# Score products with the low parts of the keys on 64 rows, head pairs on opposite halves of the array

## The chip, the cores and the metric

The kernel runs on one core of one Trainium2 chip. The metric is the device time of one execution in microseconds; three executions of the kernel before took 2033.07, 2031.86 and 2033.2 us, median 2033.07. The core's engines are TensorE (PE; its weight loads are listed apart as PEld), VectorE (DVE), ScalarE (ACT), GpSimd (POOL) and SyncE (SP), each with an instruction stream of its own. Matmul results go to PSUM, whose banks hold 512 float32 values per partition; other data lies in SBUF.

## The reference

One layer of a decoder block, 2048 positions, width 1024, float32. One projection of the normalized input gives the inputs of a gated short convolution, the queries, keys and values of a sliding-window attention (16 query heads, 4 key/value heads, head width 64, window 128), and gates. The change touches only the scores of the attention:

```python
    q = rms_norm(q.reshape(b, s, N_Q_HEADS, HEAD_DIM), q_norm_g)
    k = rms_norm(k.reshape(b, s, N_KV_HEADS, HEAD_DIM), k_norm_g)
    ...
    scores = jnp.einsum('bnqhgd,bnkhd->bnhgqk', qb.astype(jnp.float32),
                        kb.astype(jnp.float32)) * scale
    ...
    valid = (diff >= 0) & (diff < WINDOW) & (k_pos >= 0)
    scores = jnp.where(valid[None, :, None, None], scores, NEG_INF)
    ...
    m = jnp.maximum(jnp.max(scores, axis=-1, keepdims=True), sink)
    p = jnp.exp(scores - m)
    p = p / (jnp.sum(p, axis=-1, keepdims=True) + jnp.exp(sink - m))
    out = jnp.einsum('bnhgqk,bnkhd->bnqhgd', p.astype(v.dtype), vb)
```

Everything else (projections, convolution, gates, output projection, residual) is as usual for such a block and stays as it was.

## The kernel before

**Precision.** TensorE multiplies in a fast type (`F32R`) that keeps fewer bits than float32. So each operand is split into a high part, rounded to that type, and a low part, what is left. The large products (L364, `product`) take three matmuls for each: high by high, high by low, low by high; low by low is dropped.

**Layout.** The 2048 positions are worked in two tiles `t` of 1024. In each, units of 256 columns of the projections run one after another (`sunit`, L364, 512-column matmuls on 128 rows into the banks X, V and Y). Between the steps of these units the kernel places other work by hand: `put(n, f)` enters a piece of work for tick `n`, and `run` (each step of a unit is a tick) issues what is due after the unit's own matmuls. The order in each engine's stream is therefore written out by the program.

**Attention.** For each tile, key/value head `j` (4) and block `b` of 128 positions (8) there is one round of attention, 64 in all. A round is spread over ticks: `att_load` at n-4, `att_scores` at n, `att_exp` at n+1, `att_norm` at n+2, `att_turn` (four transposes, L779) at n+4, `att_values` (L809) at n+7, `att_out` at n+8. In the first half of a tile's rounds they are 5.25 ticks apart, in the second half 3.25.

**Queries and keys.** A key/value head serves four query heads, in two pairs `c` (the pair of 256-column halves `i` in `fin_q`), and in a pair two heads `e`. `fin_q` splits the queries into `hi` and `lo` and stores them by POOL's queue into `q2d`: `hi` in rows 0 to 63 (`LH`), `lo` in rows 64 to 127 (`UH`), the 64 rows being the head's 64 dimensions. `kd` holds the keys' high part (`l = 0`) and low part (`l = 1`), each written twice, to rows 0 to 63 and to rows 64 to 127. One matmul on 128 rows with `l = 0` thus gives q_hi k_hi + q_lo k_hi, and with `l = 1` it gives q_hi k_lo + q_lo k_lo.

**Scores.** `att_scores` makes eight matmuls, for `h` (half block of 64 positions), `c` and `l`, each with 128 columns of weights (64 positions times two heads) and 192 moving columns (keys of the window). Each matmul has its weight load, also where two in a row use the same weights. The result `sp` is one tile of two PSUM banks, indexed `[h, c]`, so that a half block has a bank. The pool `ps_s` has one buffer: the next round's first score matmul waits until the exponentials of this one have read theirs. Then VectorE writes the masked part (`copy_predicated`, L748; L744 and L746 in the rounds without earlier keys), takes the maximum (L750) and a few small steps, and ScalarE takes the exponentials, four of 128 columns (L763).

**Two small matmuls** in the beginning use fewer rows of the array: L163 (`prep_gain`, 8 rows, between the warming matmuls `clear`, L1098) and L168 (`prep_cols`, 42 rows).

Of the kernel before, what the change touches and what calls it, by code (L numbers as in the profile page):

```python
# [11 lines left out]
AF = mybir.ActivationFunctionType  # L12
ALU = mybir.AluOpType
AX = mybir.AxisListType

P = 128
# [9 lines left out]
HD = 64  # L26
# [12 lines left out]
LH, UH = slice(0, HD), slice(HD, P)  # L39
HALVES = (LH, UH)  # L40
# [3 lines left out]
def block_kernel(  # L44
# [15 lines left out]
    nc = tc.nc  # L60
# [18 lines left out]
    def slot(shape, dt, name):  # L79
        return big.tile(shape, dt, tag="big", name=name)  # L80
# [37 lines left out]
    for h in range(2):  # L118
        nc.gpsimd.affine_select(
            out=mask_f[:, h, :], in_=ones[:, 0:HD], pattern=[[1, HD]], compare_op=ALU.is_gt,  # L120
# [4 lines left out]
    negc = consts.tile([P, HD], F32, name="negc")  # L125
# [17 lines left out]
    rows = slot([NR, P], F32, "rows")  # L143
# [65 lines left out]
    def add(o, a, b, eng=None):  # L209
        return (eng or nc.vector).tensor_tensor(out=o, in0=a, in1=b, op=ALU.add)  # L210
# [4 lines left out]
    def mul(o, a, b, eng=None):  # L215
        return (eng or nc.vector).tensor_tensor(out=o, in0=a, in1=b, op=ALU.mult)
# [213 lines left out]
    def into(dst, val):  # L430
        if isinstance(val, tuple):
            add(dst, *val)
        else:
            nc.scalar.copy(dst, val)
# [115 lines left out]
    def put(n, f):  # L550
        at.setdefault(max(n, tick[0] + 1), []).append(f)
# [17 lines left out]
    def turn4(src, name):  # L569
        pt = mbank(name)  # L570
        for b in range(HB):
            nc.tensor.transpose(pt[:, b, :], src[:, b * P : (b + 1) * P], ident)
        return pt

    def head_square(pt, name):
        sq = pt.rearrange("p b q -> p (b q)")
        nc.scalar.activation(out=sq, in_=sq, func=AF.Square)
        return sq

    def head_reduce(sq, ss, n):  # L580
        nc.vector.tensor_reduce(
            out=ss[:, n * 8 : (n + 1) * 8], in_=sq.rearrange("p (h d) -> p h d", d=HD), axis=AX.X, op=ALU.add)

    def head_rms(ss, name):
        ms = small.tile([P, 32], F32, tag="sm", name=f"{name}_ms")
        nc.vector.tensor_scalar(out=ms, in0=ss, scalar1=1.0 / HD, scalar2=EPS, op0=ALU.mult, op1=ALU.add)
        return rsqrt(ms, 32, name)
# [3 lines left out]
    def fin_q(t, j):  # L591
        ss = small.tile([P, 32], F32, tag="ss", bufs=3, name=f"qss{t}_{j}")
        left = [4]

        def fin(i, q, val):
            nm = f"q{t}_{j}_{i}_{q}"
            qt = slot([P, H], F32, f"{nm}_t")
            into(qt, val)
            hi, lo = slot([P, H], F32R, f"{nm}_h"), slot([P, H], F32R, f"{nm}_l")
            nc.scalar.activation(out=hi, in_=qt, func=AF.Copy, scale=gqk)  # L600
            nc.vector.scalar_tensor_tensor(
                out=lo, in0=qt, scalar=gqk, in1=hi.bitcast(F32), op0=ALU.mult, op1=ALU.subtract)
            for e in range(2):
                for half, src in ((LH, hi), (UH, lo)):
                    nc.gpsimd.dma_start(
                        q2d[t][j][half, q * 2 * HB : (q + 1) * 2 * HB, i, e, :],
                        src[HALVES[e]].bitcast(F32).rearrange("p (b x) -> p b x", x=HD))

            def sums():
                sq = head_square(turn4(qt, f"pt{nm}"), nm)  # L610
                put(tick[0] + 1, lambda: reduce(sq))

            def reduce(sq):
                head_reduce(sq, ss, 2 * i + q)
                left[0] -= 1
                if left[0] == 0:
                    put(tick[0] + 1, rms)

            put(tick[0] + 1, sums)

        def rms():
            r = head_rms(ss, f"q{t}_{j}")

            rq = consts.tile([P, 2, HB, 2, 2], F32, tag="rq", bufs=4, name=f"rq{t}_{j}")
            rv = r.rearrange("p (c q b e) -> p q b c e", c=2, q=2, e=2)
            for e in range(2):
                for h in range(2):
                    nc.vector.tensor_copy(rq[HALVES[e], :, :, h, :], rv[HALVES[h], :, :, :, e])
            rqs[t, j] = rq

        return fin
# [75 lines left out]

    def att_load(t, j, b):  # L710
        nm = f"{t}_{j}_{b}"
        gb = t * NB + b
        q2 = slot([P, 2, 2, P], F32R, f"q2_{nm}")
        nc.sync.dma_start(
            q2.bitcast(F32).rearrange("p h c x -> p (h c x)"),
            q2d[t][j][:, 2 * b : 2 * b + 2].rearrange("p h c e x -> p (h c e x)"))
        k2 = slot([P, 2, 2 * P], F32R, f"k2_{nm}")
        if b > 0:
            nc.sync.dma_start(k2.bitcast(F32), kd[t][j, :, :, (b - 1) * P : (b + 1) * P])
        else:  # L720
            nc.sync.dma_start(k2[:, :, P:].bitcast(F32), kd[t][j, :, :, 0:P])
            if gb > 0:
                nc.sync.dma_start(k2[:, :, :P].bitcast(F32), kd[t - 1][j, :, :, T - P : T])
        v2 = slot([P, 4, P], F32R, f"v2_{nm}")
        nc.sync.dma_start(v2.bitcast(F32), vd[gb, :, :, j, :])
        return q2, k2, v2

    def att_scores(t, j, b, ld):
        first = t * NB + b == 0
        nm = f"{t}_{j}_{b}"  # L730
        q2, k2, _ = ld
        rv = rqs[t, j][:, b // HB, b % HB]
        sp = ps_s.tile([P, 2, 2, 2 * P], F32, tag="s", name=f"s{nm}")
        for h in range(2):
            skip = (2 - h) * HD if first else 0
            for c in range(2):
                for l in range(2):
                    nc.tensor.matmul(  # L738
                        sp[:, h, c, skip : 3 * HD], lhsT=q2[:, h, c, :],
                        rhs=k2[:, l, h * HD + skip : h * HD + 3 * HD], start=l == 0, stop=l == 1)  # L740
        sg = sp.rearrange("p h c k -> p (h c) k")
        m = mask_i.unsqueeze(1).to_broadcast([P, G, HD])
        if first:
            nc.vector.copy_predicated(  # L744
                sg[:, :, 2 * HD : 3 * HD], m, negc.unsqueeze(1).to_broadcast([P, G, HD]))
            nc.vector.tensor_copy(sg[:, 0:2, HD : 2 * HD], negc.unsqueeze(1).to_broadcast([P, 2, HD]))  # L746
        else:
            nc.vector.copy_predicated(sg[:, :, 2 * HD : 3 * HD], m, sg[:, :, 0:HD])  # L748
        st = small.tile([P, 6, G], F32, tag="st", name=f"st{nm}")
        nc.vector.tensor_reduce(out=st[:, 0], in_=sg[:, :, HD : 3 * HD], axis=AX.X, op=ALU.max)  # L750
        mul(st[:, 5].rearrange("p (h c) -> p h c", c=2), st[:, 0].rearrange("p (h c) -> p h c", c=2), rv)
        nc.vector.scalar_tensor_tensor(
            out=st[:, 1], in0=st[:, 5], scalar=-1.0, in1=nsink_r[:, j].rearrange("p h c -> p (h c)"),
            op0=ALU.mult, op1=ALU.min)
        add(st[:, 2], sink_r[:, j].rearrange("p h c -> p (h c)"), st[:, 1])
        return sg, st, rv

    def att_exp(t, j, b, got):
        sg, st, rv = got
        nc.scalar.activation(out=st[:, 3], in_=st[:, 2], func=AF.Exp)  # L760
        p = slot([P, G, P], F32, f"p{t}_{j}_{b}")
        for i in range(G):
            nc.scalar.activation(  # L763
                out=p[:, i, :], in_=sg[:, i, HD : 3 * HD], func=AF.Exp, bias=st[:, 1, i : i + 1],
                scale=rv[:, i // 2, i % 2 : i % 2 + 1], accum_out=st[:, 4, i : i + 1])
        return p, st

# [308 lines left out]
    def x_state(t):  # L1076
        return state.setdefault(t, {"raw": {}, "ops": {}, "x": {}, "ss": {}})
# [3 lines left out]
    st = x_state(0)  # L1081
# [250 lines left out]
```

## Time and profile before

| what | value |
|---|---|
| median of three executions | 2033.07 us |
| profiled execution, its own time | 2032.55 us |
| its span, first to last instruction | 2030.8 us |
| granted TensorE clock, mean | 0.999 |
| first and last start of a score matmul | 166.3 and 1529.1 us |
| a score matmul (L738), shortest, median, longest | 192, 273, 358 ns |
| a score weight load, shortest, median, longest | 186, 192, 192 ns |
| masked copy (L748), median | 422 ns |
| maximum (L750), median | 691 ns |
| one exponential (L763), median | 454 ns |
| waits of the score line for the exponentials (L763) | 8.1 us, 13 times |

A span's length is counted from the first to the last instruction, and the execution's time holds a little more. In a timeline a row gives the start, the length, the engine, the line, the operation, what it writes and reads, its shape and how many instructions were merged; in brackets stands idle time ahead of it and what ended it. The first shape of a matmul is the array's part in use (`128*128`, rows by columns), the second the moving data. Matmuls are pipelined: the recorded length of one runs beyond the start of the next, so that what one holds TensorE for is the distance between starts. A weight load overlaps the matmul ahead of it.

### The profile page before, as it was taken

Reading aid. Unit: us, or ns where it says so; the run is one execution under the profiler, and the core shown is the slowest. Engines: PE = TensorE matmul, PEld = TensorE weight load, DVE = VectorE, ACT = ScalarE, POOL = GpSimd, SP = SyncE. Lnnn points to the kernel's source line nnn. Section 1 sums busy time; section 2 is a strip of 40 time slices with the busy share of each in tenths; the row PEclk is TensorE's granted clock in tenths of the full one; section 3 lists DMA queues with packets and bytes.
Section 4 is the critical chain, followed back from the end, with each engine's and each line's share of the span. In section 5 each row is a group of like instructions: output and inputs, shape, how many; then the busy total and the mean of one; then the engine's idle time right before and its main releaser. Section 6 shows DMA issues by size and latency. Waiting matters only on the chain.

```text
span 2030.8 us, 27523 instructions
## 1 busy us (share of the span) xinstructions
PE 2002.3 (99%) x9488; PEld 1664.3 (82%) x9488; DVE 1385.3 (68%) x2360; ACT 936.9 (46%) x1847; POOL 429.2 (21%) x597
## 2 busy tenths in 40 slices
PE   8999999999999999999999999999999999999999
PEld 6787888888888887888878888888888887888887
DVE  6877787787675555348768887787776656356654
ACT  6554455456664333244545544455665334212321
POOL 1873222222321000000277222222332000100000
PEclk9999999999999999999999999999999999999999
DMA  6794424445555534664498434445555443765553
GB/s 177 223 241 137 131 83 122 133 131 173 156 173 164 176 110 148 230 221 154 126 255 215 128 100 138 128 122 168 162 177 173 148 146 129 249 214 167 174 171 109
DMA packets 339594, 329.15 MB, mean 162 GB/s; under 512 B 21804, under 2 KB 260448, under 8 KB 339456
## 3 DMA queue, kind: packets, MB, share of 16 engines
q1 hardware_dynamic: 321984, 276.37, 43.9%
q0 software_dynamic: 17456, 51.04, 9.2%
q8 instruction: 75, 1.23, 0.2%
q14 instruction: 63, 0.52, 0.1%
q10 hardware_dynamic: 16, 0.00, 0.0%
HBM read 217.61 MB, written 109.71 MB: 161 GB/s over the span
## 4 chain that ended last, share of the span: by engine, by line
PE 71%; DVE 4%; ACT 3%; issue 3%; DMA 1%; POOL 1%; SPq 0%; POOLq 0%; DVEq 0%; ACTq 0%
PE Y L364 21%; PE yb L938 9%; PE ya L938 8%; PE Vcv L364 2%; PE Xcv L364 2%; PE Xza L364 2%; PE Vz L364 2%; PE Vo L364 2%; PE Xo L364 2%; PE Xz L364 2%; PE Vza L364 2%; PE s L738 2%; PE Xgb L364 2%; PE po L809 1%; PE Xga L364 1%
## 5 line engine op out<-in xcount | busy, mean ns | idle before, releaser
L792 POOL TENSOR_SCALAR_AFFINE_SELECT xh<-xh 64x512 fp32r<-64x512 f32 x64 | 69.4, 1085 | 644.7 <-DVE xl L784 477.6
L763 ACT ACTIVATE p<-s,st,rq 128x128 f32<-128x128 f32 x256 | 113.5, 453 | 0.6
L699 POOL DMA_DIRECT2D vd<-v x112 | 69.4, 626 | 197.3 <-DVE v L207 186.4
L210 DVE TENSOR_TENSOR o<-po,o 64x256 f32<-64x256 f32 x128 | 53.7, 420 | 67.4 <-ACT o L820 61.2
L971 DVE SCALAR_TENSOR_TENSOR tha<-tha,ya 128x512 f32<-128x512 f32 x32 | 22.0, 687 | 100.8 <-PE ya L938 93.9
L820 ACT COPY o<-po 64x256 f32<-64x256 f32 x128 | 47.0, 367 | 83.6 <-DVE o L210 82.1
L938 PE MATMUL ya<-opa,wya_0h 128*128 128x512 f32 x256 | 79.5, 391 | 2.4 <-ACT opa L206 1.9
L364 PE MATMUL Xcv<-oph,wcv_ah 128*128 128x512 f32 x256 | 80.1, 394 | 0.0
L938 PE MATMUL yb<-opb,wyb_0h 128*128 128x512 f32 x256 | 79.4, 391 | 0.0
L938 PE MATMUL yb<-opb,wyb_1h 128*128 128x512 f32 x256 | 79.4, 391 | 0.0
L938 PE MATMUL ya<-opa,wya_1h 128*128 128x512 f32 x256 | 78.8, 389 | 0.0
L738 PEld LDWEIGHTS s<-k,q 128*128 128x128 f32 x512 | 65.6, 191 | 9.0 <-ACT p L763 5.4
L206 ACT CAST opb<-ocr 128x512 fp32r<-128x512 f32 x32 | 19.9, 621 | 111.5 <-DMA ocr<-ocd 109.8
L784 DVE TENSOR_TENSOR xl<-pt,xh 128x512 fp32r<-128x512 f32 x64 | 44.1, 690 | 39.7 <-ACT yp L783 33.9
L738 PE MATMUL s<-k,q 128*128 128x192 f32 (+2 forms) x512 | 67.2, 274 | 2.9 <-ACT p L763 2.7
L991 DVE SCALAR_TENSOR_TENSOR thb<-thb,yb 128x512 f32<-128x512 f32 x32 | 21.9, 686 | 55.2 <-PE yb L938 53.5
L938 PEld LDWEIGHTS ya<-opa,wya_0h 128*128 128x128 f32 x256 | 48.0, 188 | 13.6 <-ACT opa L206 2.8
L858 DVE SCALAR_TENSOR_TENSOR y<-u,cols,y 128x512 f32<-128x512 f32 x64 | 50.1, 784 | 10.6 <-ACT y L851 8.6
L1025 POOL DMA_DIRECT2D wo<-in_w_out x16 | 8.7, 544 | 226.1 <-DVE opb L207 209.7
L938 PEld LDWEIGHTS ya<-opa,wya_1h 128*128 128x128 f32 x256 | 48.1, 188 | 10.0
L792 POOL TENSOR_SCALAR_AFFINE_SELECT yp<-xl 64x512 fp32r<-64x512 f32 x64 | 55.3, 864 | 3.1
L938 PEld LDWEIGHTS yb<-opb,wyb_1h 128*128 128x128 f32 x256 | 47.6, 188 | 9.6
(583 smaller groups left out, 6246.3 us busy)
## 6 DMA issues: line engine op xcount, KB each, us to landing
wcv_raw<-in_w_in SPq DMA_DIRECT2D x64, 256.0 KB, 4.6
q<-q2d SPq DMA_DIRECT2D x64, 256.0 KB, 3.7
v<-vd SPq DMA_DIRECT2D x64, 256.0 KB, 4.4
gd<-th SPq DMA_DIRECT2D x64, 256.0 KB, 2.2
k<-kd SPq DMA_DIRECT2D x56, 256.0 KB, 4.4
vd<-v POOLq DMA_DIRECT2D x96, 128.0 KB, 3.6
wq_raw<-in_w_in SPq DMA_DIRECT2D x32, 256.0 KB, 4.3
q2d<-q_h POOLq DMA_DIRECT2D x64, 128.0 KB, 4.9
```

Of the source, the lines that this page charges most:

```text
L210: return (eng or nc.vector).tensor_tensor(out=o, in0=a, in1=b, op=ALU.add)
L364: nc.tensor.matmul(ps, lhsT=w[:, j, :], rhs=b[:, m, :], start=start and j == 0 and i == 0, stop=j == KP - 1 and i == 2, skip_group_check=n ...
L699: nc.gpsimd.dma_start(to.rearrange("b p h d -> p b h d"), v[half].bitcast(F32).rearrange("p b e l d -> p b e (l d)"))
L738: nc.tensor.matmul(sp[:, h, c, skip : 3 * HD], lhsT=q2[:, h, c, :], rhs=k2[:, l, h * HD + skip : h * HD + 3 * HD], start=l == 0, stop=l == 1)
L763: nc.scalar.activation(out=p[:, i, :], in_=sg[:, i, HD : 3 * HD], func=AF.Exp, bias=st[:, 1, i : i + 1], scale=rv[:, i // 2, i % 2 : i % 2 ...
L784: nc.vector.tensor_tensor(out=xl, in0=pt, in1=xh.bitcast(F32), op=ALU.subtract)
L792: nc.gpsimd.affine_select(out=d4, in_=s4, pattern=[[0, 2 * G], [-sg, HD]], compare_op=ALU.is_gt if prev else ALU.is_ge, fill=0.0, base=0, ...
L820: nc.scalar.copy(ov, pov[oth, :, :, e, :])
L858: nc.vector.scalar_tensor_tensor(out=y, in0=u[:, h * H + i : h * H + i + H], scalar=tap(i, k), in1=y, op0=ALU.mult, op1=ALU.add)
L938: nc.tensor.matmul(ps, lhsT=w[:, j, cs], rhs=o[:, m, :], start=p == 0 and j == 0 and i == 0, stop=p == 1 and j == KP - 1 and i == 2)
L971: nc.vector.scalar_tensor_tensor(out=m, in0=m, scalar=1.0, in1=ps, op0=ALU.add, op1=ALU.mult)
L991: nc.vector.scalar_tensor_tensor(out=m, in0=m, scalar=1.0, in1=ps, op0=ALU.add, op1=ALU.mult)
```

## The change

Which half of the rows holds a query's high part now depends on the pair: rows 0 to 63 for pair 0, rows 64 to 127 for pair 1. The matmuls with the keys' high parts stay on 128 rows. Those with the low parts use only the 64 rows that hold the queries' high part, so q_lo k_lo is no longer computed. The four high ones come first, then the four low ones, whose pairs `c` alternate between the lower and the upper rows. The result's banks go by pair instead of half block, and what reads the result is indexed to match. Only the first matmul into each bank carries the start flag. The exponentials keep their order over `i`, so they now alternate between the banks.

```diff
-                for half, src in ((LH, hi), (UH, lo)):
+                for half, src in ((HALVES[i], hi), (HALVES[1 - i], lo)):
                     nc.gpsimd.dma_start(
                         q2d[t][j][half, q * 2 * HB : (q + 1) * 2 * HB, i, e, :],
...
-        for h in range(2):
-            skip = (2 - h) * HD if first else 0
-            for c in range(2):
-                for l in range(2):
+        for l in range(2):
+            for h in range(2):
+                skip = (2 - h) * HD if first else 0
+                for c in range(2):
+                    rows = HALVES[c] if l else slice(0, P)
                     nc.tensor.matmul(
-                        sp[:, h, c, skip : 3 * HD], lhsT=q2[:, h, c, :],
-                        rhs=k2[:, l, h * HD + skip : h * HD + 3 * HD], start=l == 0, stop=l == 1)
-        sg = sp.rearrange("p h c k -> p (h c) k")
+                        sp[:, c, h, skip : 3 * HD], lhsT=q2[rows, h, c, :],
+                        rhs=k2[rows, l, h * HD + skip : h * HD + 3 * HD],
+                        start=l == 0 and h == 0, stop=l == 1, skip_group_check=True)
+        sg = sp.rearrange("p c h k -> p (c h) k")
...
-            nc.vector.tensor_copy(sg[:, 0:2, HD : 2 * HD], negc.unsqueeze(1).to_broadcast([P, 2, HD]))
+            nc.vector.tensor_copy(sp[:, :, 0, HD : 2 * HD], negc.unsqueeze(1).to_broadcast([P, 2, HD]))
...
-        nc.vector.tensor_reduce(out=st[:, 0], in_=sg[:, :, HD : 3 * HD], axis=AX.X, op=ALU.max)
+        nc.vector.tensor_reduce(
+            out=st[:, 0].rearrange("p (h c) -> p c h", c=2), in_=sp[:, :, :, HD : 3 * HD],
+            axis=AX.X, op=ALU.max)
...
-        return sg, st, rv
+        return sp, st, rv
...
-        sg, st, rv = got
+        sp, st, rv = got
...
-                out=p[:, i, :], in_=sg[:, i, HD : 3 * HD], func=AF.Exp, bias=st[:, 1, i : i + 1],
+                out=p[:, i, :], in_=sp[:, i % 2, i // 2, HD : 3 * HD], func=AF.Exp, bias=st[:, 1, i : i + 1],
```

## The prediction

> **What bounds the kernel now.** I read the busy shares first, then the chain that ended last, then the rows of the line that is changed.
>
> ```profile
> span 2030.8 us, 27523 instructions
> PE 2002.3 (99%) x9488; PEld 1664.3 (82%) x9488; DVE 1385.3 (68%) x2360; ACT 936.9 (46%) x1847; POOL 429.2 (21%) x597
> PE 71%; DVE 4%; ACT 3%; issue 3%; DMA 1%; POOL 1%; SPq 0%; POOLq 0%; DVEq 0%; ACTq 0%
> L738 PEld LDWEIGHTS s<-k,q 128*128 128x128 f32 x512 | 65.6, 191 | 9.0 <-ACT p L763 5.4
> L738 PE MATMUL s<-k,q 128*128 128x192 f32 (+2 forms) x512 | 67.2, 274 | 2.9 <-ACT p L763 2.7
> ```
>
> TensorE is busy 99% of the span and leads the chain; VectorE has 32% free and ScalarE 54%. What counts is how long the score products (L738, 512 matmuls in 64 blocks of 8) hold TensorE. A busy time can't say this, since matmuls overlap; the distance between starts can. So next I read TensorE's timeline around one block, and around one that had to wait.
>
> ```profile
> 318.58 0.61 PE L364 MATMUL Vcv<-oph,wcv_th 128*128 128x512 f32 x2
> 319.03 0.39 PE L364 MATMUL Vcv<-oph,wcv_tl 128*128 128x512 f32 x1
> 319.26 1.03 PE L738 MATMUL s<-k,q 128*128 128x192 f32 x8
> 320.13 0.65 PE L364 MATMUL Y<-oph,wcv_d 128*128 128x512 f32 x2
> ...
> 490.13 1.14 PE L738 MATMUL s<-k,q 128*128 128x192 f32 x8 [0.34 <-ACT p L763]
> ```
>
> A 512-column matmul is followed by the next after 0.23 us (319.03 to 319.26). Three in 0.68 us (318.58 plus the one at 319.03, to 319.26) give 0.227, so 192 columns stream in 192/512 of that, 0.085. But eight score products take 0.87 (319.26 to 320.13), and the two products behind them take 0.65 where others take 0.61 to 0.63, another 0.02 to 0.03: 0.896 in all, or 0.112 each. They are not bound by streaming but by the weight load, one per matmul. The block at 490.13 shows its length: there TensorE stood waiting, no weights were loaded ahead, and the block is 0.11 longer. **A weight load of this type takes 0.11 us; in a running stream it hides under the matmul ahead of it.**
>
> **The change, part by part.** Four of eight products (the low parts of the keys) go from 128 rows to 64. Numbers of matmuls, loads and columns stay. Two things can differ: products on opposite row halves may run side by side, and TensorE passes from 128-row to 64-row work and back once per block. Before, every block was 128 rows throughout.
>
> *The passage.* The trace has two matmuls with fewer rows, both tiny: one of 8 rows (L163) and one of 42 (L168). I read TensorE and its loads around them, and four transposes with and without a wait ahead of them.
>
> ```profile
> 10.02 0.86 PE L1098 MATMUL Y<-zero 128*128 128x512 f32 x3
> 10.80 0.22 PE L163 MATMUL ptg<-ident,rows_g 8*128 8x8 f32 x1
> 10.96 0.97 PE L1098 MATMUL Y<-zero 128*128 128x512 f32 x3
> ...
> 10.80 0.13 PEld L163 LDWEIGHTS ptg<-ident,rows_g 8*128 8x128 f32 x1 [0.37 <-issue]
> ...
> 10.96 0.50 PE L1098 MATMUL Y<-zero 128*128 128x512 f32 x1
> ...
> 41.12 0.39 PE L1098 MATMUL Y<-zero 128*128 128x512 f32 x1
> 41.44 0.25 PE L168 MATMUL pt<-ident,rows 42*128 42x42 f32 x1
> 41.62 0.55 PE L480 MATMUL pth<-ident,x 128*128 128x128 f32 x3
> ...
> 23.12 0.60 PE L480 MATMUL Y<-ident,x 128*128 128x128 f32 x4
> ...
> 37.87 0.66 PE L572 MATMUL ptk<-ident,k_t 128*128 128x128 f32 x4 [0.66 <-ACT k_t L434]
> ```
>
> The third 512-column matmul of the 10.02 row starts at 10.48 (two steps of 0.23 on), so its stream is out at 10.71. The 8-row load does not start under it but at 10.80, 0.09 later. At 41.12 the same: stream out at 41.35, 42-row load at 41.44, again 0.09. On the way back, the next 128-row load starts at 10.96, 0.16 (0.153 before rounding) after the tiny load; that load, of the transposes' kind, takes 0.06 when nothing hides it (0.66 against 0.60 for four), the 8 columns next to nothing, so again about 0.09 of empty array. The matmul at 10.96 then lasts 0.50 instead of 0.39: it waits 0.11 for its own load. So **each passage costs 0.09 in which the array runs empty, plus 0.11 for a load that nothing hides**. A change of data type isn't what does it: the transposes of another type follow 512-column products everywhere else after 0.23.
>
> The Trainium skill (TensorEngine Tiling (Array Packing), Tiling Modes) says that switching between tilings, not between tiles of one tiling, drains the engine. The trace agrees with its 0.09; the page gives no length. Without that rule and these rows, the sum would be rival 2's.
>
> *The products in between.* Four full products first: starts at 0, 0.09, 0.20, 0.31 (the first step is 0.085, its two loads lying ahead; then 0.112 each); the fourth has streamed at 0.40. Passage 0.09 + 0.11: first half product at 0.60. How the four half products follow is in no row. Bounds: from a gain in which a pair costs no more than one full product, 0.112, to none, 0.112 each; nothing in the rows suggests that a half load takes longer than a full one (0.13 for 8 rows against 0.19 for 128 of the costlier type). I take one load per pair: two half loads on opposite rows write the very cells that one full load writes in 0.11, the two products write different banks, and the order alternates the halves, so each pair is ready together. For the second of a pair I add 0.03 as a guess at its later issue. First pair at 0.60 and 0.63, second at 0.71 and 0.74, streamed at 0.82; passage 0.20; the next L364 product streams at 1.02.
>
> **Sum.** 1.02 - 0.896 = +0.12 us per block, x64 = +7.9. In parts: 0.40 for the four full products, 0.22 for the four half ones, 0.40 for the two passages. Profiled execution 2032.55 + 7.9 = **2040** (span 2038.7, with 1.7 around it); the median of the runs shown, 2033.07, is 0.5 above that execution.
>
> The Trainium skill (TensorE: Matmul & The Clock Gate, LDWEIGHTS) says a load's time goes by its columns and not its rows, so half the rows save nothing by themselves. If loads came singly, that gives rival 1's sum; side by side, mine.
>
> *The rest costs nothing.* The masked copy (L748), the maximum (L750, 0.69 us) and the exponentials (L763, 0.45 each) handle the same elements in another order, on engines at 68% and 46%, with TensorE's products of the next steps beside them; without that cover a few per cent on 0.69 would be 0.02 per block, 1.3 in all. The stores of the queries on POOL's queue are as many and as large; only target halves swap. No wait is added on any queue. What is late is the block's masked copy, by about 0.1; behind it wait the exponentials and, since the score tile has one buffer, the next block's first product (8.1 us in 13 waits now). There the delay is passed on, not absorbed: the wait runs from these very products. Few other waits on TensorE could swallow some; I allow 0.5 us.
>
> **Rivals.**
> 1. *Half loads come one after another.* For: every load in the trace follows the one before it, 0.112 apart. Against: all those went to the same 128 rows. Four half products then take 3 x 0.112 + 0.085 = 0.42: 0.60 + 0.42 + 0.20 = 1.22, +0.32 per block, x64 = +20.6: **2053**.
> 2. *Faster: no passage cost.* Loads run ahead across the border as they do between full products, and pairs go side by side: 6 x 0.112 in place of 8, -0.224 x 64 = -14.3: **2018**. For: the only passages in the trace are tiny transposes early on, one of them (L168) with semaphores of its own ahead. Against: the 0.09 shows in both, and on the way out, where nothing was waited for. It decides once a round trip costs less than 0.22 more than the stream; the rows above give it 0.34.
> 3. *The change doesn't do what it says*: half products treated as full ones, loads in line, no passage: 8 x 0.112 as before, **2032.5**.
> 4. *Side by side, but the second pair's loads wait until the first pair has streamed*: 0.085 more, x64 = 5.4: **2046**. This is the upper end of my own case.
>
> **How the numbers follow.** My case with 4 as its upper end: 0.53, range 2037 to 2046 (the lower end without the 0.03 and with 0.5 absorbed). Rival 1: 0.26. Rival 2: 0.11. Rival 3, or a passage partly covered: 0.10. A measurement of this kernel tells 0.2%, 4 us, from no change: 2029 to 2037.1. Below that lies rival 2: faster 0.11. Inside lie rival 3 and the low edge of my case, 0.05: same 0.15. The rest, 0.74, slower. The range is 2033 to 2055: it takes in my case, rival 1 and half of rival 3, and leaves out rival 2 and some 0.06 at the ends, 0.17.
>
> **What would show it.** In TensorE's timeline, half products carry 64 rows. Right: loads of the first half product and of the first product behind the block start some 0.09 after the stream ahead has ended; the two halves of a pair start within 0.05, pairs 0.11 apart; a block holds TensorE about 1.02. Rival 1: half products 0.11 apart, a block at 1.22. Rival 2: loads start under the last full product, a block at about 0.67. Wrong altogether: L748 or L763 lengthen by tenths, or the time moves outside these blocks.

## The result and the profile after

The changed kernel took 2036.91 us (median of 9 runs, 2034.91 to 2040.45) against 2032.03 for the kernel before (9 runs, 2030.39 to 2033.26): a ratio of 1.0025, 95% interval 1.0014 to 1.0035. By the ratio that is 5.1 us slower, 2.8 to 7.1; the medians lie 4.9 apart. The forecast was slower by 7.9, with 2040. The measured time stands 0.1 below the range that the forecast gave its own case, 2037 to 2046, and inside its wider range.

First the page of the changed kernel: span, busy shares, chain, and the rows of the score line, which is now L742.

```profile
span 2034.0 us, 27523 instructions
PE 2009.7 (99%) x9488; PEld 1658.9 (82%) x9488; DVE 1385.6 (68%) x2360; ACT 936.2 (46%) x1847; POOL 428.3 (21%) x597
PE 87%; DVE 4%; ACT 3%; DMA 2%; POOL 2%; issue 1%; SPq 0%; DVEq 0%; ACTq 0%; POOLq 0%
L742 PEld LDWEIGHTS s<-k,q 128*128 128x128 f32 (+1 forms) x512 | 56.3, 188 | 14.5 <-ACT p L770 4.2
L742 PE MATMUL s<-k,q 128*128 128x192 f32 (+3 forms) x512 | 64.5, 294 | 2.0 <-ACT p L770 2.0
```

The other engines' busy times are those of before to 1 us. The masked copy (422 ns), the maximum (691) and one exponential (454) kept their median lengths. The score loads' busy time fell by 9.3 us, as loads now overlap each other, yet the idle time of the load unit ahead of them rose from 9.0 to 14.5: that is where passages would show. The chain's shares can't be set against those of before: the chain is a sample of one path, and 87% against 71% is no 16% more work.

Now TensorE's timeline around one block of the changed kernel, then its weight loads in four narrow windows of the same block. The half products are those with `64*128`.

```profile
182.33 0.62 PE L364 MATMUL Vcv<-oph,wcv_th 128*128 128x512 f32 x2
182.79 0.39 PE L364 MATMUL Vcv<-oph,wcv_tl 128*128 128x512 f32 x1
183.02 0.98 PE L742 MATMUL s<-k,q 128*128 128x192 f32 x8
183.93 0.73 PE L364 MATMUL Y<-oph,wcv_d 128*128 128x512 f32 x2
```
```profile
182.79 1.03 PEld L742 LDWEIGHTS s<-k,q 128*128 128x128 f32 x8
...
183.53 0.19 PEld L742 LDWEIGHTS s<-k,q 64*128 64x128 f32 x2
...
183.64 0.19 PEld L742 LDWEIGHTS s<-k,q 64*128 64x128 f32 x2
...
183.93 0.19 PEld L364 LDWEIGHTS Y<-oph,wcv_d 128*128 128x128 f32 x1
```

The fourth full product starts 0.313 after the first (this and the next numbers are start times of the trace to the nanosecond), so it has streamed at 183.02 + 0.40 = 183.42, by the forecast's 0.085 for 192 columns. The first half loads come at 183.53, both in one row 0.19 long, which is the length of one load: they run side by side, 0.004 apart. The second pair of loads follows at 183.64, 0.11 later. The second pair streams from 0.708 to 0.793 after the block's start, that is to 183.81, and the load of the next full product comes 0.12 later, at 183.93. It is not hidden: the two L364 products behind the block last 0.73 in place of the 0.65 behind an old block.

From its first product to the second product behind it, this block takes 0.913 + 0.335 = 1.248 us; it took 0.871 + 0.252 = 1.123. **64 x 0.125 = 8.0 us** in the blocks, of which the end of the run shows 5.1. The block is a typical one: both kernels issue the same matmuls in the same places but for the order inside a block, and 62 of the 64 blocks (the other two are touched by a stretch at half clock, see the last section) are together 7.8 us longer than before, 0.126 each.

### The profile page after: what moved, and what is told of

The parts are those of the page before. It is cut to its first block, busy times and chain, and to the rows that moved or that the text cites. A ratio compares the mean times of both kernels' runs of the same rounds, so it can differ in the third digit from the quotient of the medians.

```text
span 2034.0 us, 27523 instructions
## 1 busy us (share of the span) xinstructions
PE 2009.7 (99%) x9488; PEld 1658.9 (82%) x9488; DVE 1385.6 (68%) x2360; ACT 936.2 (46%) x1847; POOL 428.3 (21%) x597
## 4 chain that ended last, share of the span: by engine, by line
PE 87%; DVE 4%; ACT 3%; DMA 2%; POOL 2%; issue 1%; SPq 0%; DVEq 0%; ACTq 0%; POOLq 0%
PE Y L364 28%; PE yb L945 9%; PE ya L945 8%; PE Xcv L364 4%; PE Vcv L364 4%; PE s L742 2%; PE Vb L364 2%; PE Xb L364 2%; PE Xza L364 2%; PE Vz L364 2%; PE Vo L364 2%; PE Xo L364 2%; PE Xz L364 2%; PE Vza L364 2%; PE po L816 2%; PE Xga L364 2%
## 5 line engine op out<-in xcount | busy, mean ns | idle before, releaser
L364 PE MATMUL Xcv<-oph,wcv_ah 128*128 128x512 f32 x256 | 80.4, 395 | 0.0
L742 PEld LDWEIGHTS s<-k,q 128*128 128x128 f32 (+1 forms) x512 | 56.3, 188 | 14.5 <-ACT p L770 4.2
L742 PE MATMUL s<-k,q 128*128 128x192 f32 (+3 forms) x512 | 64.5, 294 | 2.0 <-ACT p L770 2.0
```

The costliest lines, as they stand in the source:

```text
L364: nc.tensor.matmul(ps, lhsT=w[:, j, :], rhs=b[:, m, :], start=start and j == 0 and i == 0, stop=j == KP - 1 and i == 2, skip_group_check=n ...
L742: nc.tensor.matmul(sp[:, c, h, skip : 3 * HD], lhsT=q2[rows, h, c, :], rhs=k2[rows, l, h * HD + skip : h * HD + 3 * HD], start=l == 0 and ...
```

## The experiments

All times are device time, medians; each ratio is to the kernel before on the same chip, with its 95% interval.

**E1, full rows.** Everything as changed (order, banks, readers), but all products on 128 rows.

```diff
-                    rows = HALVES[c] if l else slice(0, P)
+                    rows = slice(0, P)
```

> The changed kernel with all eight score products on 128 rows; the order, the banks by pair and the readers stay as changed. Theory (two passages between 128 and 64 rows per block cost 0.425 us, the pairs win back 0.30 against the old stream, 0.125 net): no passage and no pair, so a block holds TensorE 0.87 to 0.90 us as before, and the time is that of before within 0.1%, 2030 to 2034. Rival (the new layout, order or banks give back the 3 us by which the measured change, 4.9, falls short of 64 x 0.125 = 8.0): 3 us below before, about 2029.

Measured: 2033.47 against 2032.74, ratio 1.0000 (0.9991 to 1.0009); a block again takes 0.871 + 0.252. Order, banks by pair and readers leave the block as it was, and the time to 2 us either way; the rival's 3 us lie outside that. The whole effect comes with the 64 rows.

**E2, both pairs on the same half.** Passages stay, the side by side goes.

```diff
-                for half, src in ((HALVES[i], hi), (HALVES[1 - i], lo)):
+                for half, src in ((LH, hi), (UH, lo)):
...
-                    rows = HALVES[c] if l else slice(0, P)
+                    rows = LH if l else slice(0, P)
```

> The high parts of both pairs of heads lie in rows 0 to 63 again, and all four half products use these rows: the passages stay, the side by side goes. Theory: the half products follow one another 0.112 apart; a block lasts 0.596 + 3 x 0.112 + 0.085 + 0.227 = 1.24 us against 0.896, and the time rises by up to 64 x 0.35 = 22 us, to 2051 to 2054. Rival (half loads overlap whatever rows they go to, or the halves save nothing): block and time as in the changed kernel, about 2037.

Measured: 2053.64, ratio 1.0098 (1.0084 to 1.0112), 20 us slower. The loads of the four half products, in one window of a block:

```profile
205.11 0.52 PEld L742 LDWEIGHTS s<-k,q 64*128 64x128 f32 x4
```

Four loads take 0.52, where four side by side in pairs took 0.30 (183.53 to 183.64 + 0.19). A block to the second product behind it takes 1.132 + 0.335 = 1.467, 0.344 over before. So the passages alone cost 0.344 per block, and the opposite halves win back 0.344 - 0.125 = 0.22, two loads' worth.

**E3, two round trips per block.**

```diff
-        for l in range(2):
-            for h in range(2):
+        for h in range(2):
+            for l in range(2):
```

> The half block is the outer loop again: two full products, two half products, and once more, so that a block passes to 64 rows and back twice. Theory: a block lasts 0.171 + 0.198 + 0.089 + 0.227 + 0.18 + 0.198 + 0.089 + 0.227 = 1.38 us against 0.896, and the time rises by 64 x 0.48 = 31 us, to 2060 to 2063. Rival (passages are cheap, something paid once per block costs the time): 1.02 per block, about 2037. If a fixed share of about four tenths of what a block gains in length were swallowed elsewhere: about 2051.

Measured: 2055.72, ratio 1.0111 (1.0098 to 1.0125), 23 us slower: between the two figures expected. The loads of one block, each row from a window of its own:

```profile
201.53 0.19 PEld L742 LDWEIGHTS s<-k,q 64*128 64x128 f32 x2
...
201.81 0.19 PEld L742 LDWEIGHTS s<-k,q 128*128 128x128 f32 x1
...
202.21 0.19 PEld L742 LDWEIGHTS s<-k,q 64*128 64x128 f32 x2
...
202.50 0.30 PEld L364 LDWEIGHTS Y<-oph,wcv_th 128*128 128x128 f32 x2
```

The first pair of full products starts at 201.24, and passages stand ahead of each of these four rows. A block to the second product behind it takes 1.259 + 0.334 = 1.593. That is 0.345 more than with one trip: the second trip costs as much as E2's passages did. The block is as expected (1.259 + 0.108 for the load that isn't hidden = 1.37 against 1.38); 64 x 0.470 = 30.1 us, of which 23 arrive (20 to 25 by the interval). So a part of what blocks gain in length is swallowed.

**E4, the change again.** The same kernel.

> The changed kernel once more, for its size: the score blocks alone give 64 x 0.125 = 8.0 us, 2040; what was measured is 4.9, 2037. If the blocks' time shows in full and the difference was chance: a ratio of 1.0035 to 1.0045. If some 3 us are swallowed on the way: 1.002 to 1.003, and the profile again shows less waiting at the same places in front of the second tile's queries.

Measured: 2038.52 against 2032.74, ratio 1.0030 (1.0018 to 1.0043), 6.1 us. The interval still holds 8.0, so this run alone doesn't settle it.

**E5, the low parts of the keys left out.** The kernel before with four products per block.

```diff
-                for l in range(2):
+                for l in range(1):
...
-                        rhs=k2[:, l, h * HD + skip : h * HD + 3 * HD], start=l == 0, stop=l == 1)
+                        rhs=k2[:, l, h * HD + skip : h * HD + 3 * HD], start=True, stop=True)
```

> The kernel before with the four products with the keys' low parts left out (q_hi k_lo and q_lo k_lo are not computed). A block loses 4 x 0.112 = 0.448 us, 64 x 0.448 = 28.7. Theory (a quarter of what the blocks gain or lose in length is made up by TensorE's other waits inside the attention rounds, which have their due times from other engines): 20 to 23 us below before, about 2011, and TensorE's waits for the values' operands (POOL), for the exponentials and for the probabilities grow by some 4 to 6 us. Rival (the blocks' time shows one for one, and the gaps so far were chance or the clock): 28 to 29 below, about 2004, with these waits unchanged.

Measured: 2011.44 against 2031.66, ratio 0.9905 (0.9890 to 0.9919), 19 us faster (16 to 22). A block to the second product behind it takes 0.424 + 0.253 = 0.677, 0.446 less: 28.5 us. About a third is missing at the end, also on the way down, so the swallowing is not chance, and the rival's 28 to 29 falls. Not being the same computation, this is no version to use.

**E6, the kernel before again**, for a second profile.

> The kernel before once more, for a second profile of it. Theory: blocks and the waits inside the attention rounds as in the first profile within 0.5 us in sum; the waits in front of the second tile's queries (3.7 us over a step's length there, 1.3 in the changed kernel's profile) vary by a microsecond or two from execution to execution and are no effect of the change. Rival: they are again at 3.7, and the change swallows them.

Measured: one execution, 2030.45. TensorE's waits by whom it waited for (us in total, times, longest), of before, of before again, of the change, of the change again, of E5 and of E3:

```profile
PE s L738 <- ACT p L763: 2.7, 4, 1.2
...
PE Y L364 <- DVE Vq L210: 2.2, 1, 2.2
PE pt L779 <- DVE p L216: 2.2, 2, 1.8
...
PE po L809 <- POOL xl L792: 1.4, 4, 0.4
PE Vcv L364 <- DVE wcv_sl L270: 1.3, 1, 1.3
...
PE Vgb L364 <- DVE wgb_sl L270: 0.8, 1, 0.8
```
```profile
PE s L738 <- ACT p L763: 2.6, 4, 1.2
PE pt L779 <- DVE p L216: 2.2, 2, 1.8
...
PE po L809 <- POOL xl L792: 1.4, 4, 0.4
PE Y L364 <- DVE Vq L210: 1.3, 1, 1.3
```
```profile
PE pt L786 <- DVE p L216: 2.0, 2, 1.8
...
PE s L742 <- ACT p L770: 2.0, 4, 1.1
...
PE Y L364 <- DVE Vq L210: 0.9, 1, 0.9
```
```profile
PE s L742 <- ACT p L770: 2.0, 4, 1.1
PE pt L786 <- DVE p L216: 2.0, 2, 1.8
...
PE Y L364 <- DVE Vq L210: 0.6, 1, 0.6
...
PE po L816 <- POOL xl L799: 0.3, 2, 0.2
```
```profile
PE s L738 <- ACT p L763: 4.6, 7, 1.6
PE pt L779 <- DVE p L216: 2.7, 2, 1.8
...
PE Vcv L364 <- DVE wcv_sl L270: 1.7, 3, 1.3
PE po L809 <- POOL xl L792: 1.6, 5, 0.4
...
PE Vgb L364 <- DVE wgb_sl L270: 1.2, 1, 1.2
PE po L809 <- POOL yp L792: 1.2, 4, 0.3
...
PE Vga L364 <- DVE wga_sl L270: 0.7, 2, 0.5
```
```profile
PE pt L786 <- DVE p L216: 1.8, 1, 1.8
...
PE s L742 <- ACT p L770: 1.2, 2, 0.7
```

Three waits inside the attention rounds (score products for the exponentials, transposes for the probabilities, values for POOL) stand at 6.3 and 6.2 us before, 4.0 and 4.3 in the changed kernel, 3.0 in E3 with the longest blocks, and 10.1 in E5 with the shortest. In E1, with the new order and banks but blocks as long as before, they stand at 6.2. They move against the blocks' length: that is a part of the swallowing, some 2 of 3 us in the change, 3 of 7 in E3 and 4 of 9 in E5, where 4 to 6 were expected. In E5 TensorE also waits longer for the low parts of weights (`wcv_sl`, `wgb_sl`, `wga_sl`), 3.6 us in place of 2.1. The wait for `Vq`, ahead of the second tile's queries, where no round is running, was 2.2 and 1.3 for the same kernel, and in E2 and E3 it was 2.2 and 2.1; it varies, and the change isn't shown to shorten it.

**E8, half products not alternating**: lower half twice, then upper half twice.

```diff
-            for h in range(2):
-                skip = (2 - h) * HD if first else 0
-                for c in range(2):
+            for h, c in ((0, 0), (1, 0), (0, 1), (1, 1)) if l else ((0, 0), (0, 1), (1, 0), (1, 1)):
+                skip = (2 - h) * HD if first else 0
+                if True:
```

> The changed kernel with the half products in another order: both on the lower rows first, then both on the upper. Theory (work on one half runs in line, 0.112 apart, and on the other half beside it, but loads keep the order of the program): the third product starts with the second, the fourth 0.112 later; a block is 0.596 + 0.112 + 0.112 + 0.085 + 0.227 = 1.13 us against 1.02, 64 x 0.11 = 7 over the changed kernel, less about a quarter: 2042 to 2045. Rivals: the upper half starts with the first product whatever the order, 1.02, 2037; or nothing overlaps unless it alternates, 1.24, 2053.

Measured: 2037.57 against 2031.66, ratio 1.0033 (1.0019 to 1.0048), and a block of 0.915 + 0.341, as in the changed kernel. The theory's part on order fell; the first rival held. The first round shows it, since its half products differ in width: the program's order is 64, 128, 64, 128 columns (lower, lower, upper, upper), and a row of the timeline tells them apart by the columns. TensorE's timeline in two narrow windows:

```profile
166.91 0.30 PE L742 MATMUL s<-k,q 64*128 64x64 f32 x2
...
167.05 0.31 PE L742 MATMUL s<-k,q 64*128 64x128 f32 x2
```

Both 64-column products start at 166.91, 0.006 apart, and both 128-column ones 0.13 later. The third of the program started ahead of the second. The other three rounds without earlier keys show the same.

## Why the prediction was right

**The passage** was the right mechanism: E1 has none and its blocks are those of before, and E2 and E3 put 0.344 and 0.345 on a round trip beyond the running stream. The forecast had 0.34, and rival 2, which needed less than 0.22, falls by that. The sizes of its parts were too low both ways. The empty array lasts 0.115 on the way in and 0.119 on the way out (0.115 there too, if counted from the later half of the last pair), not the 0.09 of the two tiny matmuls; with an unhidden load of 0.108 that is 0.22 to 0.23 per passage against 0.20. The Trainium skill (TensorEngine Tiling (Array Packing), Tiling Modes) has the drain without a length; these rows give it one.

**The pairs** did what the forecast assumed without a row for it: one load's time per pair, the halves 0.003 to 0.004 apart instead of the guessed 0.03, so that from the first pair's stream to the end of the second 0.172 pass (0.621 to 0.793), not 0.22. That one load per pair was right was the forecast's choice between bounds, not a reading. E2 shows what rival 1 would have been: its block came out at +0.344 (the rival had 0.32), its time at 2053.6 (the rival had 2053, with a cheaper block and nothing swallowed, so that the times agree by luck). Rival 4, the second pair's loads waiting, falls by the loads at 183.64. Rival 3, no passage and loads in line, falls with the 0.115 ahead of the `64*128` loads and with their coming in pairs.

**The block**: 0.398 (four full) + 0.115 + 0.108 (passage in) + 0.172 (pairs) + 0.119 + 0.108 (passage out) = 1.02, which the forecast had, by luck: its two passages were 0.05 too cheap in sum (0.40 against 0.45), and its pairs 0.05 too dear (0.22 against 0.17).

**From block to end**: this term was mis-sized. "Few other waits on TensorE could swallow some; I allow 0.5 us": the listed waits inside the rounds gave back 1.9 to 2.3 us. It was also wrong that the delay ahead of the next score products "is passed on, not absorbed": the score products' wait for the exponentials fell from 2.7 to 2.0. That other engines' due times hold those waits, so that a longer block eats into them, is argued; that they move against the block's length is shown, down in the change and in E3, up in E5, and unmoved in E1. With 8.0 in the blocks and some 2 swallowed, 6 remain; measured were 5.1 and 6.1. The first median, 2036.91, lies below the 2037.1 up to which the forecast would have called a single time unchanged; the interval over nine runs and the blocks tell it apart.

What stays open is the last microsecond or so. Single profiles differ by more than that for reasons that the change doesn't touch: the wait for `Vq`, and stretches at half clock (below). And E3 lacks 7 us of its 30, of which the three listed waits give 3.2 (6.2 to 3.0); E5 lacks 9 of its 28.5, of which they and the waits for the weights' low parts give 5.4. Where the rest, some 4 us in each, went was not followed up.

## What to carry to other kernels

Row packing pays by the pair and is paid for by the round trip. Here a pair won 0.11 us and a round trip cost 0.34, so a stretch on 64 rows needs more than three pairs to break even, and two were in it. That count is an estimate from E2 and the change; no run had more than two pairs in a stretch. Before packing, count how many packed pairs stand between two passages, and look whether the products are bound by their loads (start distance 0.112 against a stream of 0.085); then the gain is the load saved, as here 0.22 for two pairs, and not the columns.

## What the runs showed of the hardware that was not expected

**Half products overtake each other.** In E8 a product on the upper rows started ahead of one on the lower rows that the program issues earlier. The Trainium skill (TensorE: Matmul & The Clock Gate, The mechanism) says that matmuls start and end in program order; between row halves the starts here did not. Alternating the halves by hand was therefore not needed in this kernel: the median block takes 1.257 us in E8 and 1.256 in the changed kernel.

**Stretches of 3.4 us at half clock** come and go between executions. The granted clock stands in the column after POOL; the first row is the kernel before, the second the changed kernel in the same stretch, the third the changed kernel later.

```profile
168.90:172.30 3.40, 3.40 (x10) 2.87 (x11) 3.40 (x5) 2.17 (x4) 3.40 (x6) 0.50 0.66 123
```
```profile
168.90:172.30 3.40, 3.40 (x15) 2.55 (x14) 3.33 (x7) 1.89 (x4) 3.40 (x6) 1.00 0.88 181
...
1409.90:1413.30 3.40, 3.40 (x13) 2.57 (x13) 2.40 (x6) 2.29 (x4) 1.40 (x3) 0.50 1.03 293
```

Ahead of the first, TensorE had waited 1.59 us; after the same wait, 1.60, the changed kernel kept its clock, and lost it at 1409.9 after a wait of 1.79, which the kernel before had too (1.78) without losing it. At a clock of 0.50 a stretch costs up to half its length, by estimate 1.7 us, a third of the effect that was to be measured.
